# Four staging tiles and a later store for the last pair's differences in the down projections

## The chip, the cores and the metric

The kernel runs on one core of one Trainium2 chip. The metric is the device time of one execution in microseconds. Five engines work side by side, each through a queue of its own in order: TensorE (PE, with its weight loads PEld), VectorE (DVE), ScalarE (ACT), GpSimd (POOL) and SyncE (SP), which here only issues DMA transfers. An instruction whose semaphore isn't up yet holds back everything behind it on its engine's queue.

## The reference, cut to what matters

A decoder trunk with two layers over 1024 tokens of width 1024, each a mixer (retention and RWKV-7 in layer 0, windowed attention in layer 1) followed by a dense SwiGLU FFN with an inner width of 2816. The change touches only the end of the FFN:

```
def swiglu(h, w_gate, w_up, w_down):
    return (jax.nn.silu(h @ w_gate) * (h @ w_up)) @ w_down
...
    n = rms_norm(h, norm2_g[layer])
    h = h + swiglu(n, ffn_w_gate[layer], ffn_w_up[layer], ffn_w_down[layer])
```

Everything is float32.

## The kernel before, in words

**Arithmetic.** Each float32 operand is split into a rounded high half and a low half (an fp32r pair): ACT casts the high half, and DVE or POOL subtracts it from the source to get the low half. `prod` (lines 1297 to 1303) then issues three matmuls per 128x128 block, high by high (L1300), high by low (L1302) and low by high (L1303). The FFN's three products are taken over 2x2 blocks with seven block products in place of eight. For the down projection the blocks of the hidden values are: first or second inner tile of a pair, by first or second half of the tokens. There are 22 inner tiles of 128, so `NP` = 11 pairs. The sums and differences of blocks that the seven products need must be formed, split and kept: those of the hidden values are called the inner differences here.

**Inner differences.** `form_down(L, p, x, ts)` (line 1432) makes four of them for pair p. Its inner function `put(i, o, a, b)` subtracts on DVE (L1437), splits the result into a staging tile `t` (cast on ACT, L462; low half on POOL or, for the last pair, on DVE, L464), and has the tile stored to DRAM as `hc[L][p, i-1]` (512 KB, L1446 on SP's queue). The order of the puts is 1, 2, 4, 3. There are two staging tiles, `ts`: puts 1 and 4 use the first, puts 2 and 3 the second. So put 4's cast has to wait until put 1's store has read the tile, and put 3's cast until put 2's store has. `stage` (line 1412) makes the eight tiles of the late FFN: two staging tiles, two for each of the two sets `xs[0]` and `xs[1]` of hidden blocks (pairs take the sets in turn), and two for raw weights.

**When.** For pairs 0 to 9 `form_down` runs in the next pair's steps of the FFN (`ffn_late`, line 1854). For the last pair, 10, it runs as `rest` inside the down projection. `down` (line 1521) goes through three groups of pairs, (0 to 3), (4 to 7) and (8 to 10). In a group there are seven products, each over four output tiles `dp`:

| product | hidden operand | weights | PSUM tiles in group 0 (in group 1 the two sets are swapped) |
|---|---|---|---|
| 1 | first tile, first tokens, loaded plain from `hid` (L1502) and split | plain block | f, f, f, y |
| 2 | difference 2, loaded ready split from `hc` (L1497) | sums made by DVE (L1518) | m, m, r, c |
| 3 | second tile, first tokens, plain | plain block | f, f, f, y |
| 4 | difference 3 | sums | m, m, r, c |
| 5 | difference 4 | plain block | m, m, r, c |
| 6 | difference 1 | first sums, `s1` | f, f, f, y |
| 7 | second tile, second tokens, plain | second sums | f, f, f, y |

The weights come as raw halves into tiles `wd0` and `wd1` (L1510, five buffers each), are summed by DVE where needed, and are cast by ACT (L1491) and their low halves taken by POOL (L1492) into a ring of six tiles (`w`, and `wr`). The hidden operands take turns in twelve tiles (`n`, `ha`), four to a product, so an operand can be loaded when the product three before it is over.

**What sets the order.** A list scheduler orders each engine's queue by a timeline of its own, with the program's order as priority, save that the DMA issues marked with `keep` stay in program order among themselves. In program order a group's loads for products 1 to 7 come first to last; the transfers listed in `self.owed` are issued between the loads for product 5 and those for product 6 (line 1583, L1584), and `rest` stands after the loads for products 6 and 7 of group 0 (line 1592). The puts are held behind the last addition of product 5 by `self.rest`. Behind them on SP's queue stand the loads of group 1:

```
            X = [self.sums8(L, p, 4, place()) for p in ps]
            while self.owed:
                self.keep(self.nc.sync.dma_start(*self.owed.pop(0)))
...
            X = [self.sums8(L, p, 1, place()) for p in ps]
            X6 = [plain(1, 2 * p + 1) for p in ps]
            self.rest = self.last_vop
            for _ in rest:
                pass
```

Already before the change, `owed` carries three stores of the last pair's hidden values and two differences of pair 9. The first reader of `hc[L][10]` is product 2 of group 2.

## Time and profile before

| what | value |
|---|---|
| median of three runs | 2300.83 us (2300.7 to 2303.07) |
| profiled execution, its own time | 2298.91 us |
| profiled execution, span of the program in it | 2296.9 us |
| granted TensorE clock, mean | 0.998 |
| PE, DVE, ACT, POOL busy | 98%, 74%, 46%, 44% of the span |
| down projection of layer 0, products 2 of group 0 to 3 of group 2 | about 1119 to 1294 us |
| down projection of layer 1, the same | about 2080 to 2256 us |

The profile is one execution. The view of busy time by windows gives, for a stretch of the span, its length and then each engine's busy time with the number of instructions that touch the stretch. The view in order of time gives start, length, engine, line, operation, output and inputs; in square brackets stands how long the engine was idle before and what released it. Matmuls overlap in it: one is shown as 0.39 us long, while the next starts 0.22 to 0.23 us after it. For SP only the issue of a transfer is shown, and the landing is given apart. `SPq` is SP's queue.

### The profile page before, as it was taken

The page shows a single profiled execution, that of the slowest core. Times are in us where ns is not written, and L with a number is a line of the kernel's source. Part 1 is how long each engine was busy: PE and PEld are TensorE (multiplying, and loading weights), DVE is VectorE, ACT ScalarE, POOL GpSimd, SP SyncE. Part 2 cuts the span into 40 slices and gives each one's busy share as a digit, 9 for nine tenths or more (in the row PEclk, how much of TensorE's full clock was granted, in tenths as well). Part 3 has the DMA queues.
Part 4 walks back from the last instruction along what each step waited for, and adds up shares of the span by engine and source line. Part 5 has one row for each costly group of instructions (what it writes and reads, how often), then busy time and mean ns, then how long its engine had stood idle before and what let it go on. Part 6 is the DMA issues. An engine that isn't in the chain of part 4 may idle for free.

```text
span 2296.9 us, 35740 instructions
## 1 busy us (share of the span) xinstructions
PE 2261.4 (98%) x13056; PEld 1808.1 (79%) x13056; DVE 1694.1 (74%) x2635; ACT 1046.4 (46%) x1947; POOL 1007.3 (44%) x796
## 2 busy tenths in 40 slices
PE   8999999999999999999999999999999999999998
PEld 6777777778878888888878887787788888888786
DVE  7877965876567268887876958857657788888766
ACT  5454544424445333334333466657744333333335
POOL 3122221212340167777768501113203677777675
PEclk9999999999999999999999999999999999999999
DMA  8566554444356555565755332133246565556663
GB/s 279 190 211 207 195 160 132 141 117 132 134 183 224 170 175 202 207 216 210 284 234 202 114 119 74 44 106 110 92 147 225 178 215 208 205 193 252 259 218 115
DMA packets 170335, 406.42 MB, mean 177 GB/s; under 512 B 43184, under 2 KB 45872, under 8 KB 170160
## 3 DMA queue, kind: packets, MB, share of 16 engines
q1 hardware_dynamic: 166752, 397.59, 50.1%
q10 hardware_dynamic: 2832, 4.45, 0.5%
q8 instruction: 104, 1.70, 0.3%
q0 software_dynamic: 576, 2.10, 0.2%
q14 instruction: 71, 0.58, 0.1%
HBM read 275.48 MB, written 123.21 MB: 174 GB/s over the span
## 4 chain that ended last, share of the span: by engine, by line
PE 76%; DVE 11%; ACT 4%; DMA 4%; issue 3%; POOL 1%; SPq 1%; DVEq 0%; ACTq 0%; POOLq 0%
PE ps_f L293 11%; PE ps_m L1300 7%; PE ps_m L1302 7%; PE ps_m L1303 7%; PE ps_m L293 6%; PE ps_f L1300 4%; PE ps_f L1302 4%; PE ps_f L1303 4%; PE ps_f L450 2%; PE ps_f L447 2%; PE ps_f L449 2%; PE ps_r L1300 2%; PE ps_c L1303 2%; PE ps_r L1302 2%; PE ps_c L1302 2%
## 5 line engine op out<-in xcount | busy, mean ns | idle before, releaser
L293 PE MATMUL ps_f<-n,w 128*128 128x512 f32 x1440 | 358.5, 402 | 9.9 <-ACT w L432 5.8
L293 PEld LDWEIGHTS ps_f<-n,w 128*128 128x128 f32 x1440 | 267.1, 189 | 83.9 <-issue 12.6
L433 POOL TENSOR_TENSOR w<-wr,w 128x512 fp32r<-128x512 f32 x63 | 86.8, 1383 | 301.3 <-ACT w L432 299.8
L432 ACT CAST w<-wr 128x512 fp32r<-128x512 f32 x231 | 141.0, 617 | 162.0 <-PE ps_f L450 54.3
L433 DVE TENSOR_TENSOR w<-wr,w 128x512 fp32r<-128x512 f32 x168 | 118.3, 707 | 62.4 <-ACT w L432 61.8
L1300 PE MATMUL ps_f<-n,w 128*128 128x512 f32 x415 | 164.2, 396 | 0.0
L1302 PE MATMUL ps_f<-n,w 128*128 128x512 f32 x415 | 162.7, 392 | 0.0
L1303 PE MATMUL ps_f<-n,w 128*128 128x512 f32 x415 | 162.5, 392 | 0.0
L433 POOL TENSOR_TENSOR w<-wq,w 128x512 fp32r<-128x512 f32 x91 | 130.3, 1443 | 31.7 <-ACT w L432 31.7
L1300 PE MATMUL ps_m<-n,w 128*128 128x512 f32 x333 | 130.5, 392 | 1.3 <-DVE u L1310 1.3
L1302 PE MATMUL ps_m<-n,w 128*128 128x512 f32 x333 | 130.2, 391 | 0.5 <-POOL n L464 0.3
L1303 PE MATMUL ps_m<-n,w 128*128 128x512 f32 x333 | 129.6, 390 | 0.0
L1310 DVE TENSOR_TENSOR nq<-ps_m,u 128x512 f32<-128x512 f32 x88 | 58.8, 684 | 92.3 <-PE ps_m L1303 92.3
L1727 POOL TENSOR_SCALAR s<-s,st 128x256 f32<-128x256 f32 (+1 forms) x32 | 30.5, 952 | 191.8 <-ACT w L432 61.0
L1492 POOL TENSOR_TENSOR w<-wd,w 128x512 fp32r<-128x512 f32 (+1 forms) x62 | 87.0, 1415 | 45.6 <-ACT w L1491 32.6
L464 POOL TENSOR_TENSOR n<-nq,n 128x512 fp32r<-128x512 f32 x60 | 100.0, 1679 | 7.6 <-ACT n L462 7.6
L1300 PEld LDWEIGHTS ps_f<-n,w 128*128 128x128 f32 x415 | 77.9, 188 | 20.2 <-issue 3.8
L1300 PE MATMUL ps_m<-cb,w 128*128 128x512 f32 x236 | 91.9, 390 | 0.3 <-DVE nq L1310 0.3
L1303 PE MATMUL ps_m<-cb,w 128*128 128x512 f32 x236 | 91.8, 389 | 0.0
L1302 PEld LDWEIGHTS ps_f<-n,w 128*128 128x128 f32 x415 | 77.9, 188 | 17.6 <-issue 2.0
L1302 PE MATMUL ps_m<-cb,w 128*128 128x512 f32 x236 | 91.8, 389 | 0.0
L1303 PEld LDWEIGHTS ps_f<-n,w 128*128 128x128 f32 x415 | 77.9, 188 | 16.8 <-issue 0.7
(521 smaller groups left out, 6489.7 us busy)
## 6 DMA issues: line engine op xcount, KB each, us to landing
hc<-n SPq DMA_DIRECT2D x84, 512.0 KB, 3.0
wsp<-w SPq DMA_DIRECT2D x54, 512.0 KB, 3.2
w<-wsp SPq DMA_DIRECT2D x54, 512.0 KB, 3.4
n<-hc SPq DMA_DIRECT2D x54, 512.0 KB, 6.6
wq<-in_w_gate SPq DMA_DIRECT2D x44, 512.0 KB, 4.5
u<-u SPq DMA_DIRECT2D x88, 256.0 KB, 2.9
ha<-hc SPq DMA_DIRECT2D x34, 512.0 KB, 6.0
hid<-n SPq DMA_DIRECT2D x66, 256.0 KB, 2.0
```

The lines of the kernel that those rows point to most:

```text
L293: i = self.nc.tensor.matmul(out, lhsT, rhs, **kw)
L432: nc.scalar.copy(hi[:, :n], raw[:, c])
L433: self.lo.tensor_tensor(out=lo[:, :n], in0=raw[:, c], in1=hi.bitcast(F32)[:, :n], op=ALU.subtract)
L447: x = nc.tensor.matmul(ps, hi, rh, start=k == 0, stop=False)
L449: y = nc.tensor.matmul(ps, hi, rl, start=False, stop=False)
L450: z = nc.tensor.matmul(ps, lo, rh, start=False, stop=k == n - 1)
L464: e.tensor_tensor(out=lo, in0=src, in1=hi.bitcast(F32), op=ALU.subtract)
L1300: i = mm(ps, hi, xh, start=first and k == 0, stop=False, skip_group_check=True)
L1302: mm(ps, hi, xl, start=False, stop=False, skip_group_check=True)
L1303: mm(ps, lo, xh, start=False, stop=last and k == len(w) - 1, skip_group_check=True)
L1310: self.last_add = V.tensor_tensor(out=o, in0=x, in1=y, op=ALU.add)
L1492: nc.gpsimd.tensor_tensor(out=lo, in0=v, in1=hi.bitcast(F32), op=ALU.subtract)
```

## The change

`stage` gives each set of hidden blocks two more names, `11s` and `12s`, for its two whole tiles. `ffn_late` returns, beside the two staging tiles, the two tiles of the set that the last pair doesn't use (pair 9's, read for the last time by pair 9's own `form_down`). For the last pair each put takes a tile of its own, `ts[i - 1]`, and its store goes to the list `owed`, whichever put it is. At that time group 0 has emptied the list already, so the four stores are issued in group 1, between its loads for product 5 and for product 6. Pairs 0 to 9 are as they were. The number of matmuls, subtractions, casts, and bytes moved is the same.

```
-        return [{nm: t[4 - 2 * i + j // 2][:, j % 2, :] for j, nm in enumerate(names)} for i in range(2)], t[:2], [
+        xs = [{nm: t[4 - 2 * i + j // 2][:, j % 2, :] for j, nm in enumerate(names)} for i in range(2)]
+        for i, x in enumerate(xs):
+            x["11s"], x["12s"] = t[4 - 2 * i : 6 - 2 * i]
+        return xs, t[:2], [
...
-            t = ts[i in (2, 3)]
+            t = ts[i - 1] if p == NP - 1 else ts[i in (2, 3)]
             self.split(o, t[:, 0, :], t[:, 1, :], p < NP - 1)
             d = (self.hc[L][p, i - 1], t.bitcast(F32))
-            if p == NP - 2 and i > 2:
+            if p == NP - 1 or p == NP - 2 and i > 2:
                 self.owed.append(d)
...
-            return xs[(NP - 1) % 2], ts, X, W
+            old = [xs[NP % 2][nm + "s"].bitcast(F32R) for nm in ("11", "12")]
+            return xs[(NP - 1) % 2], ts + old, X, W
```

## The prediction

> **What bounds the kernel now.** I read the page first: the span, and how full TensorE is.

> ```profile
> span 2296.9 us, 35740 instructions
> ...
> PE 2261.4 (98%) x13056; PEld 1808.1 (79%) x13056; DVE 1694.1 (74%) x2635; ACT 1046.4 (46%) x1947; POOL 1007.3 (44%) x796
> ```

> PE is the bound, and no matmul goes away. So the change can only be worth the holes that it closes in PE's stream, and cost the holes that it opens. I looked for holes next, with the view of busy time by windows, cut at the borders of the products. In layer 0 the rows are products 5, 6 and 7 of group 0, then the first 108 matmuls of group 1 (products 1 and 2 and a quarter of 3), and last products 1 to 3 of group 2, which have 108 matmuls too. Below come the last two stretches for layer 1, with the 180 matmuls between them:

> ```profile
> 1152.40:1163.28 10.88, 10.88 (x49) 9.01 (x48) 10.57 (x10) 3.53 (x6) 9.40 (x7) 1.00 0.00 0
> 1163.28:1174.16 10.88, 10.88 (x49) 9.01 (x48) 10.69 (x13) 3.53 (x6) 5.32 (x3) 1.00 0.20 82
> 1174.16:1185.04 10.88, 10.88 (x49) 9.01 (x48) 3.67 (x7) 3.73 (x6) 2.77 (x2) 1.00 0.87 319
> 1185.04:1211.78 26.74, 25.72 (x110) 19.89 (x108) 23.25 (x25) 11.69 (x21) 19.92 (x14) 1.00 0.91 353
> ...
> 1263.46:1287.94 24.48, 24.48 (x110) 20.27 (x108) 21.49 (x26) 11.46 (x21) 14.21 (x14) 1.00 0.65 223
> ```

> ```profile
> 2146.61:2174.02 27.41, 25.74 (x110) 19.88 (x108) 22.86 (x25) 11.82 (x22) 20.06 (x14) 1.00 0.90 350
> 2174.02:2214.84 40.82, 40.82 (x181) 33.78 (x180) 25.14 (x31) 13.49 (x22) 34.54 (x23) 1.00 0.60 214
> ...
> 2225.72:2250.20 24.48, 24.48 (x109) 20.27 (x108) 19.85 (x24) 11.95 (x22) 14.13 (x14) 1.00 0.63 223
> ```

> The columns are length, then busy time and count of PE, PEld, DVE, ACT and POOL, then clock, DMA share and GB/s. Count by the weight loads: 108 matmuls take 24.48 us in group 2 of both layers, the pace of a full PE. The first 108 matmuls of group 1 take 26.74 and 27.41 us. So **the start of group 1 loses 2.26 us in layer 0 and 2.93 us in layer 1, together 5.19 us**. The start of group 2 loses nothing, and the clock is 1.00 throughout. The DMA columns give the hint: the DMA engines stand idle in product 5 (share 0.00), nearly so in product 6 (0.20), and then run full (0.87, 0.91) just when group 1 begins.

> Then I asked who fed PE late there (rows in order of time, PE of both layers, then what stands behind it):

> ```profile
> 1198.99 0.50 PE L1300 MATMUL ps_f<-ha,w 128*128 128x512 f32 x1 [0.93 <-ACT w L1491]
> ...
> 2147.33 0.50 PE L1302 MATMUL ps_m<-n,w 128*128 128x512 f32 x1 [0.33 <-POOL n L464]
> ...
> 2161.24 0.50 PE L1300 MATMUL ps_f<-ha,w 128*128 128x512 f32 x1 [1.25 <-ACT w L1491]
> ```

> ```profile
> 1189.19 0.92 DVE L1518 TENSOR_TENSOR ws<-wd 128x512 f32<-128x512 f32 x1 [2.10 <-DMA wd<-in_w_down]
> ...
> 1198.31 0.62 ACT L1491 CAST w<-ws 128x512 fp32r<-128x512 f32 x1 [2.40 <-DVE ws L1518]
> ```

> PE waited for a cast, the cast for a sum of weights on DVE, and the first such sum for its raw weights from DRAM. In layer 1 PE also waited for the low half of a plain operand. All of it is late loading. SP's queue says why:

> ```profile
> 1142.44 2.56 SPq L1502 DMA_DIRECT2D hr<-hid  x4
> 1168.54 8.40 SPq L1446 DMA_DIRECT2D hc<-n  x4
> 1177.00 0.42 SPq L1510 DMA_DIRECT2D wd<-in_w_down  x1
> 1177.52 2.16 SPq L1502 DMA_DIRECT2D hr<-hid  x4
> ```

> ```profile
> SPq L1446 <- DVE n L464: 30.0, 4, 23.1
> ```

> After the last loads of group 0, issued by 1145.00, SP stands for 23.1 us at the first of the last pair's four stores, and 30.0 us at all four, waiting for their low halves. Group 1's loads stand behind them and start at 1177.00, eight microseconds before group 1 does. Last, the casts of the last pair:

> ```profile
> 1171.21 0.62 ACT L462 CAST n<-nq 128x512 fp32r<-128x512 f32 x1 [1.61 <-DMA hc<-n]
> 1175.26 0.62 ACT L462 CAST n<-nq 128x512 fp32r<-128x512 f32 x1 [3.42 <-DMA hc<-n]
> ```

> These are puts 4 and 3, held by the stores of puts 1 and 2, whose tiles they overwrite.

> **The change part by part.**

> *Four tiles.* The two waits on ACT (1.61 and 3.42 us) go. PE ran full across them (10.88 us of 10.88 in products 6 and 7), so by themselves they are worth nothing to the end; they only let the last store, and SP, go some microseconds earlier. The tiles taken over belong to pair 9's set, which nothing reads after pair 9's differences; I count no new wait.

> *Stores leave SP's place before group 1.* This is the term that counts. SP then goes from 1145.00 straight to group 1's loads. What can hold them now? The first weight half has a free fifth buffer: at once. The four plain operands need the raw tiles of product 7's operands, the last of which DVE reads here:

> ```profile
> 1155.87 1.78 DVE L464 TENSOR_TENSOR n<-hr,n 128x512 fp32r<-128x512 f32 x1
> ```

> That is early in product 5. The other three first halves were last read in product 3. The second halves free up with product 5's casts. The differences for product 2 come free when product 6 ends, 1174.16. So the weights and plain operands land by about 1165 (my estimate from those borders), where now their issue begins at 1177.00: twenty microseconds ahead of use. DMA has room: shares of 0.00 and 0.20 there. The nearest case in the trace is group 2, whose loads weren't held by such stores: 0 us lost in 24.48 us, in both layers. Bounds for the gain are therefore 0 and 5.19 us; I take 5.19, the row of group 2 being the nearest, and keep both ends.

> *Stores reissued in group 1.* Rows of SP's queue around their new place in layer 0, and what such stores took elsewhere:

> ```profile
> 1206.79 2.36 SPq L1497 DMA_DIRECT2D ha<-hc  x4
> 1218.09 1.72 SPq L1497 DMA_DIRECT2D n<-hc  x3
> ```

> ```profile
> L1584 SPq DMA_DIRECT2D hc<-n x4: 490/557/640, 1132.6 to 2094.7; - x4
> ...
> DMA to landing us min/median/max: 7.5/8.0/9.1
> ```

> They go in after the four loads at 1206.79, which end at 1209.15. The queue then stands idle until 1218.09, that is 8.94 us. Four issues at up to 0.64 us take 2.56 us of it. Landing takes at most about 9.1 us, so by 1221. Their first reader is product 2 of group 2, after 1271 (products 1 to 3 start at 1263.46, and the first is a third of their 24.48 us). Cost 0. If that cover were gone, the four issues would put 2.56 us in front of product 6's loads, which have the rest of products 4 and 5 as slack. Nothing is queued behind a wait there: the halves have been ready since group 0.

> *Work that follows the loads.* Casts, splits and sums of group 1 come earlier: two low halves of product 1's operands on DVE and two on POOL move from the very start of group 1 into product 6 of group 0, where DVE is nearly full (10.69 of 10.88 us). Rows of DVE there, and PE's next use of the second bank:

> ```profile
> 1166.63 0.69 DVE L1437 TENSOR_TENSOR nq<-n,n 128x512 f32<-128x512 f32 x1
> ...
> 1168.44 1.78 DVE L1437 TENSOR_TENSOR nq<-n,nq 128x512 f32<-128x512 f32 x1
> ...
> 1172.44 0.68 DVE L1518 TENSOR_TENSOR h<-h,ps_f 128x512 f32<-128x512 f32 x1
> ```

> ```profile
> 1176.88 0.39 PE L1300 MATMUL ps_f<-n,w 128*128 128x512 f32 x1
> ```

> The same subtraction takes 0.69 us or 1.78 us. Product 7 may write its second bank (1176.88) only once DVE has read it (1173.12): a margin of 3.76 us. Two moved halves at up to 1.78 us use 3.56 us of it. I take 0 as the cost; the ends are 0 and the slower rival's price below.

> *Sum.* 0 − 5.19 + 0 + 0 = −5.19 us. The profiled execution took 2298.91 us, of which 2296.9 us are the span; that would be 2293.7 us. The median of the runs lies 1.92 us above that execution, so the forecast for it is 2300.83 − 5.19 = **2295.6 us**, −0.23%. What PE gains in layer 0 is passed on, since all later work depends on it and PE is 98% busy.

> [...]

> **The rivals.**

> *Only part of the stall goes.* DVE may not sum group 1's weights before product 7's additions (the code holds them behind these), so the two waits for a cast could stay even with early loads. They are 0.93 and 1.25 us in the rows above, 2.18 us. For it: that order is in the code. Against it: group 2 has it too and lost nothing, though its operands are three pairs wide, not four. Time: −(5.19 − 2.18) = −3.0, so 2297.8 us.

> *The loads stay late, or the gain comes out elsewhere.* The change moves the stores but the loads wait for something that now hides behind them, such as the raw tiles or the ring of twelve; then the start of group 1 is as before. For it: DMA's idle stretch in product 5 proves only the stores' wait, not what comes next. Against: the borders worked out above. Time: 0, so 2300.8 us.

> *Slower: DVE's queue in product 6.* The queues are ordered anew. If the moved halves and the two puts that no longer wait stand ahead of DVE's read of the second bank, PE waits at product 7. Price: DVE has 10.69 us of work in product 6; with two halves more at 1.78 us and its nine short instructions stretched by 1.09 us each (1.78 − 0.69) it has 24.1 us, against 10.88 + 3.76 = 14.6 us of room: 9.4 us per layer. At the other end, the two halves alone, 3.56 us, it still fits. The point that decides is 3.76 us of added delay before that read; a net loss starts where both layers wait over 5.19 us together, so at about 6.4 us of added delay. Between that break-even, 2.6 us per layer, and the upper end, 9.4 us, the middle is 6.0 us: 12.0 − 5.19 = +6.8, so 2307.6 us. Upper end: 18.8 − 5.19 = +13.6, so 2314.4 us. For it: DVE is full there, and the order is the scheduler's. Against it: in group 1, the same splits before group 2 cost nothing (40.82 us for 180 matmuls is the full pace), though there are no puts among them.

> **How the numbers follow.** A measurement of this kernel tells about 0.2% from no change, 4.6 us, that is under 2296.2 or over 2305.4 us. Chances: forecast 0.42, part 0.24, none 0.16, slower 0.18. The forecast lies just beyond the bound, so 0.02 of it falls short. Faster 0.40, same 0.02 + 0.24 + 0.16 = 0.42, slower 0.18. The range reaches from 2293.0 (the forecast with 2.6 us of spread, about the 2.4 us that the three runs differ by) to 2303.0 (no gain, with 2.2 us), and leaves out the slower rival. Since cases of both signs are in, the forecast's own range is 2293.0 to 2297.0 us.

> **What would show it.** Right: SP's first load of group 1 right after 1145 in layer 0 and before product 5 ends in layer 1; DMA share well above 0.00 in product 5; no ACT wait for a store of `hc`; 108 matmuls in about 24.5 us at the start of group 1; four stores of `hc` issued by L1584 in group 1. Wrong: the same 26.7 and 27.4 us there (loads still late); waits for ACT casts but none for POOL's halves (the part); a new wait of PE on DVE in product 7 (the slower rival); or a difference outside the down projections, which would mean that the reordering of queues outweighs all of this.

## The result and the profile after

| | before | changed |
|---|---|---|
| median, first measurement, 5 runs each | 2300.83 us | 2292.58 us (2290.52 to 2295.7) |
| ratio to before, 95% interval | | 0.9961 [0.9949, 0.9972] |
| median, second measurement, 35 and 11 runs | 2299.89 us | 2293.56 us |
| ratio to before, 95% interval | | 0.9974 [0.9963, 0.9984] |
| profiled execution, its own time and its span | 2298.91, 2296.9 us | 2295.7, 2293.9 us |

The kernel became faster, by 8.25 us in the first measurement and about 6 us in the second. The forecast was 2295.6 us and the range ended at 2293.0, so the first measurement lies 0.42 us below it. Single runs of the kernel before scatter over 10 us (2296.01 to 2306.28 in 35 runs), so I rest what follows on stretches of the profile, which repeat much better, and use the medians to check their sum.

First the page of the changed kernel: the same matmuls, a little more of the span filled by PE.

```profile
span 2293.9 us, 35742 instructions
...
PE 2261.0 (99%) x13056; PEld 1810.2 (79%) x13056; DVE 1698.6 (74%) x2635; ACT 1047.1 (46%) x1947; POOL 1006.5 (44%) x796
```

Next the view of busy time by windows of the changed kernel. Layer 0's products 5, 6 and 7 of group 0, the first 108 matmuls of group 1 and of group 2; in the last row the first 108 matmuls of layer 1's group 1. Columns as in the prediction.

```profile
1156.03:1166.91 10.88, 10.88 (x50) 9.01 (x48) 10.58 (x10) 5.26 (x9) 9.87 (x8) 1.00 0.55 166
1166.91:1177.79 10.88, 10.88 (x50) 9.01 (x48) 10.85 (x14) 5.01 (x10) 6.68 (x5) 1.00 0.76 290
1177.79:1188.67 10.88, 10.88 (x50) 9.01 (x48) 10.69 (x11) 4.44 (x8) 8.33 (x7) 1.00 0.77 270
1188.67:1213.15 24.48, 24.48 (x110) 20.27 (x108) 23.46 (x24) 8.11 (x15) 17.37 (x11) 1.00 0.41 130
1264.83:1289.31 24.48, 24.48 (x110) 20.27 (x108) 22.03 (x27) 11.35 (x22) 14.25 (x14) 1.00 0.65 224
2146.59:2171.07 24.48, 24.48 (x109) 20.27 (x108) 23.05 (x25) 7.91 (x15) 17.55 (x11) 1.00 0.44 132
```

The start of group 1 now takes 24.48 us in both layers, the pace of group 2, to the hundredth. It took 26.74 and 27.41. The DMA share (last column but one) shows why: 0.55 in product 5, where it was 0.00, and 0.41 at the start of group 1, where it was 0.91. The transfers moved ahead of their use.

SP's queue in the changed kernel, around the end of group 0 in layer 0, and the place where the stores went:

```profile
1145.95 2.51 SPq L1505 DMA_DIRECT2D hr<-hid  x4
1148.50 0.47 SPq L1513 DMA_DIRECT2D wd<-in_w_down  x1
1157.36 4.74 SPq L1505 DMA_DIRECT2D hr<-hid  x4
1162.14 4.38 SPq L1513 DMA_DIRECT2D wd<-in_w_down  x7
1175.94 2.36 SPq L1500 DMA_DIRECT2D ha<-hc  x4
```

```profile
1208.58 2.36 SPq L1500 DMA_DIRECT2D ha<-hc  x4
1211.03 2.89 SPq L1587 DMA_DIRECT2D hc<-n  x4
1219.46 2.36 SPq L1500 DMA_DIRECT2D n<-hc  x4
```

All of this execution runs some 3.6 us later than that of before (product 5 begins at 1156.03, not 1152.40; the last section says why). The first weight half goes out right behind the last loads of group 0, at 1148.50. The other loads of product 1 wait for free tiles, no longer for stores, and are all issued by 1166.52, which is 22 us before group 1 begins; in before they began 8 us before it. Product 2's differences follow at 1175.94, when tiles of the ring come free. In layer 1 it is the same. The four stores take 2.89 us of SP's idle time at 1211. SP's waits at this line (the second row, 0.4 us in each layer, belongs to the last pair's stores, the first to a store of group 0 in layer 1), and how long all stores by this line took to land:

```profile
SPq L1587 <- DVE h L1521: 0.9, 1, 0.9
SPq L1587 <- DVE y L1521: 0.8, 2, 0.4
```

```profile
DMA to landing us min/median/max: 7.7/8.2/9.9
```

So SP loses 0.4 us at them, in time in which it is idle anyway. The last one is issued at 1213.49 and in DRAM by 1223. The loads that bring the differences back for product 2 of group 2, one for each of its three pairs, go out 20 us later at the earliest:

```profile
1243.26 0.33 SPq L1500 DMA_DIRECT2D ha<-hc  x1
1252.10 1.00 SPq L1500 DMA_DIRECT2D n<-hc  x2
```

Last, the last two casts of the four puts on ACT, and DVE's reads of product 6's second and third bank, then the read of the third bank in before:

```profile
1175.83 0.62 ACT L462 CAST n<-nq 128x512 fp32r<-128x512 f32 x1 [1.87 <-DVE nq L1440]
1176.88 0.61 ACT L462 CAST n<-nq 128x512 fp32r<-128x512 f32 x1
```

```profile
1176.92 0.68 DVE L1521 TENSOR_TENSOR h<-h,ps_f 128x512 f32<-128x512 f32 x1
...
1180.53 0.68 DVE L1521 TENSOR_TENSOR h<-h,ps_f 128x512 f32<-128x512 f32 x1
```

```profile
1173.64 0.68 DVE L1518 TENSOR_TENSOR h<-h,ps_f 128x512 f32<-128x512 f32 x1
```

No cast of the last pair waits for a store any more; one waits for its own subtraction. DVE's read of the second bank ends at 1177.60, that is 10.69 us after product 6 began (1166.91). In before it ended 9.84 us after (1173.12 and 1163.28). The work that moved used up 0.85 of the 3.76 us of margin there. At the third bank it used up more: its read ends at 1181.21, and product 7 writes this bank from 1183.23 on, a margin of 2.02 us, where before had 5.28 (1174.32 and 1179.60). Layer 1 has 2.02 us there too.

The full sum of what differs: 2.26 us in layer 0 and 2.93 in layer 1, which I had, and **1.38 us at a place that I did not have**, in layer 1's late FFN, long before its down projection. Here is that stretch in before, then in the changed kernel:

```profile
1950.06:2000.08 50.02, 48.75 (x214) 39.82 (x213) 43.33 (x46) 18.04 (x31) 36.09 (x25) 1.00 0.55 198
```

```profile
1951.49:2000.13 48.64, 48.64 (x215) 39.82 (x213) 41.98 (x46) 18.21 (x31) 36.46 (x25) 1.00 0.58 202
```

The same 213 matmuls, in the same order on every engine, and PE lost 1.27 us in before and nothing after. DVE's busy time fell from 43.33 to 41.98 us for the same 46 instructions. The puts that run there are those of earlier pairs, which the change leaves as they were.

### The profile page after: what moved, and what is told of

It reads as the page before. It is cut to its first block, busy times and chain, and to the rows that moved or that the text cites. A ratio compares the mean times of both kernels' runs of the same rounds, so it can differ in the third digit from the quotient of the medians.

```text
span 2293.9 us, 35742 instructions
## 1 busy us (share of the span) xinstructions
PE 2261.0 (99%) x13056; PEld 1810.2 (79%) x13056; DVE 1698.6 (74%) x2635; ACT 1047.1 (46%) x1947; POOL 1006.5 (44%) x796
## 4 chain that ended last, share of the span: by engine, by line
PE 77%; DVE 10%; ACT 5%; DMA 3%; issue 3%; SPq 1%; POOL 1%; DVEq 0%; ACTq 0%; POOLq 0%
PE ps_f L293 9%; PE ps_m L1300 7%; PE ps_m L1303 7%; PE ps_m L1302 7%; PE ps_m L293 6%; PE ps_f L1300 5%; PE ps_f L1302 5%; PE ps_f L1303 5%; PE ps_f L450 2%; PE ps_f L447 2%; PE ps_f L449 2%; PE ps_r L1300 2%; PE ps_c L1303 2%; PE ps_r L1303 2%; PE ps_r L1302 2%
## 5 line engine op out<-in xcount | busy, mean ns | idle before, releaser
L1300 PE MATMUL ps_f<-n,w 128*128 128x512 f32 x415 | 164.2, 396 | 0.0
L1302 PE MATMUL ps_f<-n,w 128*128 128x512 f32 x415 | 162.7, 392 | 0.0
L1300 PE MATMUL ps_m<-n,w 128*128 128x512 f32 x333 | 130.4, 392 | 0.0
L1302 PE MATMUL ps_m<-n,w 128*128 128x512 f32 x333 | 129.6, 389 | 0.0
L464 POOL TENSOR_TENSOR n<-nq,n 128x512 fp32r<-128x512 f32 x60 | 100.1, 1681 | 7.6 <-ACT n L462 7.6
L1300 PEld LDWEIGHTS ps_f<-n,w 128*128 128x128 f32 x415 | 77.9, 188 | 20.2 <-issue 3.8
L1300 PE MATMUL ps_m<-cb,w 128*128 128x512 f32 x236 | 91.9, 389 | 0.4 <-DVE nq L1310 0.4
L1302 PEld LDWEIGHTS ps_f<-n,w 128*128 128x128 f32 x415 | 77.9, 188 | 17.7 <-issue 2.0
L1302 PE MATMUL ps_m<-cb,w 128*128 128x512 f32 x236 | 91.8, 389 | 0.0
```

What stands on the lines that cost most here:

```text
L464: e.tensor_tensor(out=lo, in0=src, in1=hi.bitcast(F32), op=ALU.subtract)
L1300: i = mm(ps, hi, xh, start=first and k == 0, stop=False, skip_group_check=True)
L1302: mm(ps, hi, xl, start=False, stop=False, skip_group_check=True)
```

## The experiments

Theory A is the prediction's: SP's queue is what matters, the four tiles are worth nothing by themselves. Rival B: the tiles matter too, because the waits that they remove stand in the chain that leads to the stores. For the 1.38 us the theories were formed on the way. The table gives medians, ratios with their intervals, and three stretches of each kernel's profile: the first 108 matmuls of group 1 in both layers, and layer 1's late FFN.

| kernel | median us (runs) | ratio to before, 95% | layer 0 | layer 1 | late FFN |
|---|---|---|---|---|---|
| before, again | 2299.99 (11) | 1.0004 [0.9995, 1.0014] | 27.04 | 27.72 | 50.01 |
| changed, again | 2293.56 (11) | 0.9974 [0.9963, 0.9984] | 24.48 | 24.48 | 48.65 |
| four tiles only | 2296.48 (11) | 0.9983 [0.9973, 0.9992] | 24.83 | 25.48 | 50.00 |
| stores on POOL's queue only | 2296.32 (12) | 0.999 [0.9981, 0.9998] | 25.46 | 26.38 | 48.67 |
| change in layer 0 only | 2296.71 (11) | 0.9988 [0.9979, 0.9997] | 24.48 | 27.48 | 48.63 |
| change in layer 1 only | 2298.72 (11) | 0.9994 [0.9985, 1.0003] | 27.19 | 24.48 | 50.04 |
| late stores only | 2293.42 (6) | 0.9971 [0.996, 0.9982] | 24.48 | 24.48 | 48.66 |
| four tiles, stores on POOL's queue | 2292.55 (6) | 0.9969 [0.9958, 0.998] | 24.48 | 24.48 | 48.66 |

**The kernel before and the changed one, again.** No edit. They show how far the stretches and the medians repeat.

> The kernel before, unchanged, timed against itself. Scatter theory (the 3 us by which the change gained more than the 5.19 us of its two stretches are chance events of single executions outside the down projections): single runs spread over 4 us or more, the median stands within 2 us of the other copy, and the profile shows such events at other places than the first profile did. Elsewhere theory (the 3 us are a standing effect of the newly ordered queues behind group 0): the first 108 matmuls of group 1 again take 26.7 and 27.4 us, and PE again waits 1.27 us for DVE in the late FFN of layer 1 at about 1962 us.

> The changed kernel a second time, on another chip run. Scatter theory: again 5 to 8 us faster, the amount not the same as the 8.25 us of the first time; 24.48 us for the first 108 matmuls of group 1 in both layers. Elsewhere theory: again 8 us faster, with the stretch between the two down projections again 1.4 us shorter than in the kernel before.

The stalls of before vary by 0.3 us between its two profiles (in the kernels with copies below, which leave them alone, they take up to 27.42 us in layer 0 and once 28.69 in layer 1), the late FFN by 0.01 us. The change repeats its stretches to 0.01 us, and its gain is smaller by the medians, 6.3 us, than in the first measurement. The stretches sum up to 6.57 us, which lies in both intervals. So each of the two theories holds in part: the 1.4 us of the late FFN are a standing effect, and what the first measurement gained beyond 6.57 us didn't come again.

**Four tiles only.** The tiles of the change, with the stores at once on SP's queue (edit against the changed kernel).

```
             t = ts[i - 1] if p == NP - 1 else ts[i in (2, 3)]
...
-            if p == NP - 1 or p == NP - 2 and i > 2:
+            if p == NP - 2 and i > 2:
```

> Four tiles, but the last pair's stores issued at once on SP's queue, ahead of group 1's loads, as before. Queue theory (the gain comes from group 1's loads no longer standing behind the stores): no ACT wait for a store any more, the four stores issued by about 3 us earlier, group 1's loads still not before 1172, so most of the loss stays: 25.3 to 26.5 us for the first 108 matmuls in layer 0, 26 to 27 us in layer 1, and 1 to 2.5 us faster in all. Tiles theory (the gain comes from the two waits of ACT): 24.5 us in both layers and 5 us or more faster.

SP's queue of this kernel in layer 0, and the two starts of group 1:

```profile
1142.38 2.51 SPq L1505 DMA_DIRECT2D hr<-hid  x4
1168.38 5.72 SPq L1449 DMA_DIRECT2D hc<-n  x4
1174.15 0.59 SPq L1513 DMA_DIRECT2D wd<-in_w_down  x1
```

```profile
1184.88:1209.71 24.83, 24.81 (x110) 20.19 (x109) 21.82 (x23) 10.81 (x20) 18.25 (x13) 1.00 0.88 345
2144.36:2169.84 25.48, 25.14 (x110) 20.04 (x108) 21.91 (x25) 11.28 (x21) 17.73 (x12) 1.00 0.90 348
```

SP still stands at the first store until 1168.38, but the four stores take 5.72 us, not 8.40, and group 1's first load goes out at 1174.15, which is 10.73 us before group 1 begins, not 8.04. These 2.69 us were enough for 1.91 and 1.93 us of the stalls. **Theory A falls in this point**: the casts' waits for stores were no loss to PE where they stood, but the longer one was a link of a chain (store of put 2, cast of put 3, its low half, its store, SP, group 1's loads) that ended in PE's stall.

**Stores on POOL's queue only.** Two tiles as in before; the last pair's stores leave SP's queue (edit against before).

```
-                (nc.gpsimd if p == NP - 2 else nc.sync).dma_start(*d)
+                (nc.gpsimd if p >= NP - 2 else nc.sync).dma_start(*d)
```

> Two tiles as before, the last pair's four stores issued at once but on POOL's queue instead of SP's. Queue theory: group 1's loads start right after 1145 in layer 0, the two ACT waits for stores stay (1.6 and 3.4 us or a little longer), and the first 108 matmuls of group 1 still take 24.5 us in both layers: 5 us faster, less what POOL loses by four issues of 0.6 us and by waiting for the last pair's low halves. Tiles theory: 26.7 and 27.4 us stay, no gain.

The first weight load on SP, the last two puts' casts on ACT, and the landing of layer 0's four stores in this kernel, then the same in before:

```profile
1143.32 0.33 SPq L1510 DMA_DIRECT2D wd<-in_w_down  x1
```

```profile
1174.06 0.62 ACT L462 CAST n<-nq 128x512 fp32r<-128x512 f32 x1 [3.67 <-DMA hc<-n]
1181.06 0.62 ACT L462 CAST n<-nq 128x512 fp32r<-128x512 f32 x1 [6.38 <-DMA hc<-n]
```

```profile
DMA to landing us min/median/max: 2.9/5.4/7.7
```

```profile
DMA to landing us min/median/max: 2.6/2.6/3.0
```

The loads are as early as in the changed kernel, and yet 0.98 us of layer 0's stall and 1.90 of layer 1's stay (25.46 and 26.38, less 24.48). Now the stores, issued from 1169.96 to 1183.55, stand among loads that went out early (SP issues eight more from 1170.40 to 1174.76), and take up to 7.7 us to land where they took 3.0 at most. That the loads slow them is my reading of these times; POOL's queue by itself isn't the reason, since before's four stores on it, for pair 9, landed in 2.9 to 3.1 us. The casts that must wait for them stand 3.67 and 6.38 us (1.61 and 3.42 in before), with group 1's casts of weights behind them on ACT's queue. So with SP's queue free the two waits still cost PE time, now through ACT's queue. The two parts alone recover 3.84 and 2.31 us, 6.15 in all, more than the 5.19 that there were: they overlap, and neither is a term that can be added.

**Both, in two other ways.** Four tiles with the stores at once on POOL's queue (edit against the changed kernel):

```
-            if p == NP - 1 or p == NP - 2 and i > 2:
+            if p == NP - 2 and i > 2:
...
-                (nc.gpsimd if p == NP - 2 else nc.sync).dma_start(*d)
+                (nc.gpsimd if p >= NP - 2 else nc.sync).dma_start(*d)
```

> Four tiles, and the four stores issued at once on POOL's queue: both parts without the later place. Both-parts theory: 24.5 us for the first 108 matmuls of group 1 in both layers, as with the change, and 5 us or more faster; no ACT wait for a store. If the later place in SP's queue matters by itself (the stores taking DMA time from group 1's loads), some of the loss stays, 25 us or more.

and two tiles with the stores in group 1 (edit against before). In this kernel two of the four stored differences are others than the reference's (puts 4 and 3 have overwritten the tiles by then), so it has no wait of a cast for a store, and its time is that of the late place alone:

```
-            if p == NP - 2 and i > 2:
+            if p == NP - 1 or p == NP - 2 and i > 2:
```

> Two tiles as before, but all four stores issued a group later on SP's queue. Queue theory alone: group 1's loads start right after 1145 and 24.5 us for its first 108 matmuls. Both-parts theory (early loads need the four tiles, since otherwise the casts of the third and fourth difference wait for the stores, and ACT's later casts behind them): these two casts wait until the stores are issued in product 2 or 3 of group 1, PE waits for casts or sums there, and the stretch takes more than 26.7 us or its loss moves into products 3 to 5; no gain or slower.

Both have 24.48 us in both layers, and their ratios, 0.9969 and 0.9971, can't be told from the changed kernel's. So the later place as such is worth nothing, nor do the four issues on POOL cost anything. What counts is that **no load of group 1 stands behind a last pair's store, and no cast waits for one**.

**One layer at a time.** The change where `L == 0` (edit against the changed kernel); the other kernel has `L == 1` in the same places:

```
-            t = ts[i - 1] if p == NP - 1 else ts[i in (2, 3)]
+            t = ts[i - 1] if p == NP - 1 and L == 0 else ts[i in (2, 3)]
...
-            if p == NP - 1 or p == NP - 2 and i > 2:
+            if p == NP - 1 and L == 0 or p == NP - 2 and i > 2:
```

> The whole change, in layer 0 alone. Queue and tiles together: 24.48 us for the first 108 matmuls of group 1 in layer 0, 27.4 us in layer 1. Standing theory (the shorter stretch in layer 1's late FFN, 48.65 for 50.0 us, is carried there from the new order in layer 0): it is 48.65 us here too, and the kernel is 2.3 + 1.4 = 3.7 us faster. Chance theory: that stretch may be 50.0 or 48.65 us, and the kernel is 2.3 us faster.

> The whole change, in layer 1 alone. 26.7 us for the first 108 matmuls of group 1 in layer 0, 24.48 us in layer 1. Standing theory: the stretch of layer 1's late FFN stays at 50.0 us, as its instructions stand before the change, and the kernel is 2.9 us faster. Chance theory: the stretch may come out at 48.65 us.

Each closes its own layer's stall and leaves the other's as it was. The late FFN of layer 1 is short with layer 0's part and long with layer 1's. So the 1.38 us come from what the change does in layer 0, some 760 us earlier.

**What in layer 0 does it?** In all long kernels ACT's cast `w<-ws` near 1950 us starts about 0.36 us after the matmul that releases it; in the short ones some 0.08 us after. Counted from ACT's first instruction (number 0, waiting instructions included), that cast is number 2367 in before and 2369 in the changed kernel, which has two waiting instructions more ahead of it. The other kernels of the table fit: 2367 in before again, with four tiles only and with layer 1 only, all long; 2369 to 2373 in the rest, all short. Late starts of 0.36 us were at the numbers 1215, 1343, 1599, 2239, 2367 and 2495 of ACT in one kernel or another, whatever instruction had the number: in before at 1215 and 2367, in the changed kernel at 2367, there the cast `w<-n` at 1949.29 (0.35 us). Theory P (position): the instruction at such a number starts late, and the change moved the number off the cast. Rival T (timing): earlier transfers of layer 0 shift what follows. To tell them apart, N copies of 128x16 into an unused tile stand on ACT at the start of layer 1's mixer, in before or in the changed kernel; up to 65 of them leave the order of everything else as it was (with 127 and more, a few neighbouring instructions of the mixer change places).

```
+        z = self.t(ap, [P, 16], "z")
+        for _ in range(N):
+            nc.scalar.copy(z, self.pv[:, :16])
         self.pk = self.pvt = None
```

> Before, with two copies of 128x16 on ACT at the start of layer 1's mixer, into a tile that nothing reads. The order of all engines is otherwise that of before. Theory (position): on ACT, an instruction whose number in the queue ends a block of 64 starts some 0.28 us late; the two copies move that from the cast of the weight sum at about 1950 us to an instruction two places earlier, as the change's additional waits do. Then layer 1's stretch from about 1950 to 2000 us takes 48.65 us, not 50.0, the stalls at the start of group 1 stay at 26.7 to 27.0 and 27.4 to 27.7 us, and the whole is about 1.4 us faster (0.9994). Rival (timing): the stretch gets shorter because the earlier loads of layer 0 shift all that follows; then two copies do nothing and it stays at 50.0 us.

> Before, with 64 such copies in the same place. Position: 64 is a whole block, so the same cast is hit again and the stretch takes 50.0 us, as in before. If merely having more ACT work in the mixer, or another phase, made the stretch shorter, it would take 48.65 us here too. The stalls at the start of group 1 stay as before.

> The changed kernel with 62 such copies in the same place: with the two additional instructions that stand ahead of the cast in the changed kernel they make a whole block of 64. Position: the stretch takes 50.0 us again, though the start of group 1 is at the full 24.48 us in both layers. Timing: the loads of layer 0 are as early as in the changed kernel, so it stays at 48.65 us.

> Before, with 65 copies on ACT at the start of layer 1's mixer. In the trace of the kernel with 64 copies one waiting instruction of ACT is gone, so the cast near 1950 us came 63 places later, not 64, and had number 2430 (62 beyond a multiple of 64); the stretch took 48.64 us. With 65 copies it comes 64 places later, number 2431 (63 beyond). Position: the cast starts late again and the stretch takes 50.0 us. Timing, or any effect of the amount of ACT work: as with 64 copies, 48.65 us.

> The changed kernel with 63 copies there. With 62 copies the cast had number 2430 and the stretch took 48.63 us; one copy more makes it 2431, again 63 beyond a multiple of 64. Position: the stretch takes 50.0 us, with the start of group 1 at 24.48 us in both layers. Timing: 48.65 us, as in the changed kernel and with 62 copies.

> Before, with 129 copies on ACT at the start of layer 1's mixer. In all traces so far ACT's late starts of about 0.36 us lie on numbers that leave 63 when divided by 128 (1215, 1343, 1599, 2239, 2367, 2495), so a block is 128 instructions, not 64; 65 copies put the cast on 2431, which leaves 127, and it wasn't late. With 129 copies the cast comes 128 places later, number 2495. Position with blocks of 128: the cast starts about 0.36 us after its release and the stretch takes 50.0 us. Timing, or the amount of ACT work: 48.65 us, as with 2, 64 and 65 copies.

> The changed kernel with 127 copies there: its cast near 1950 us has number 2369 without them, and with 126 places more 2495. Position with blocks of 128: the stretch takes 50.0 us although the start of group 1 stays at 24.48 us in both layers. Timing: 48.65 us, as in the changed kernel without copies.

> Before, with 130 copies on ACT at the start of layer 1's mixer. With 129 copies two waiting instructions went, so the cast had number 2494 and the waiting instruction behind it 2495; that one came 0.30 us after the cast's start, where with 65 copies it came 0.02 us after. With one copy more the cast itself has number 2495. Position with blocks of 128: the cast starts about 0.36 us after its release and the stretch takes 50.0 us. Timing, or the amount of ACT work: 48.6 us, as with 129 copies.

> The changed kernel with 128 copies there: with 127 the cast had number 2494 and the stretch took 48.63 us. Position with blocks of 128: the cast has number 2495 and the stretch takes 50.0 us, although the start of group 1 stays at 24.48 us in both layers. Timing: 48.63 us, as with 127 copies.

| kernel, N | number of the cast | late FFN us | group 1, layers 0 and 1 |
|---|---|---|---|
| before, 0 | 2367 = 18 x 128 + 63 | 50.02 | 26.74, 27.41 |
| before, 2 | 2369 | 48.65 | 26.84, 27.28 |
| before, 64 | 2430 | 48.64 | 27.42, 27.41 |
| before, 65 | 2431 = 18 x 128 + 127 | 48.67 | 26.83, 27.24 |
| before, 129 | 2494 | 48.61 | 27.08, 28.69 |
| before, 130 | 2495 = 19 x 128 + 63 | 50.03 | 27.08, 27.64 |
| changed, 0 | 2369 | 48.64 | 24.48, 24.48 |
| changed, 62 | 2430 | 48.63 | 24.48, 24.48 |
| changed, 63 | 2431 = 18 x 128 + 127 | 48.66 | 24.48, 24.48 |
| changed, 127 | 2494 | 48.63 | 24.48, 24.48 |
| changed, 128 | 2495 = 19 x 128 + 63 | 50.01 | 24.48, 24.48 |

Two copies bring the gain without the change (their median of 10 runs, 0.9994 [0.9985, 1.0004], is too coarse to tell 1.4 us). Then I missed twice. I had taken the step for 64; with 65 and 63 copies the cast stood exactly 64 places behind 2367, on 2431, and started on time, so steps of 64 fell. The numbers above fit 128 as well. And the copies took one or two waiting instructions with them, which I counted only after the runs with 64, 62, 129 and 127. With 130 and 128 copies the cast has number 2495, and the long stretch is back in both kernels, though in the changed one the start of group 1 stays at 24.48 us. One copy less, and it is short. T says nothing of this. **P holds, with steps of 128.**

How 0.28 us become 1.38: the late FFN by windows in the changed kernel with 127 copies and with 128, then rows of the first (second fence) and of the second (third fence), by engine.

```profile
1950.64:1999.27 48.63, 48.63 (x215) 39.82 (x213) 41.98 (x46) 18.16 (x31) 36.46 (x25) 1.00 0.57 203
...
1950.72:2000.73 50.01, 48.74 (x215) 39.82 (x213) 43.33 (x46) 18.03 (x31) 36.09 (x25) 1.00 0.54 197
```

```profile
1950.90 0.63 ACT L432 CAST w<-ws 128x512 fp32r<-128x512 f32 x1 [2.11 <-PE ps_m L1303]
...
1951.95 1.50 DVE L1440 TENSOR_TENSOR nq<-n,nq 128x512 f32<-128x512 f32 x1
...
1956.78 0.68 DVE L1440 TENSOR_TENSOR nq<-n 128x512 f32<-128x512 f32 x1
...
1956.81 1.80 POOL L433 TENSOR_TENSOR w<-ws,w 128x512 fp32r<-128x512 f32 x1 [0.50 <-ACT w L432]
```

```profile
1951.26 0.62 ACT L432 CAST w<-ws 128x512 fp32r<-128x512 f32 x1 [2.39 <-PE ps_m L1303]
...
1952.03 1.77 DVE L1440 TENSOR_TENSOR nq<-n,nq 128x512 f32<-128x512 f32 x1
...
1957.12 1.77 DVE L1440 TENSOR_TENSOR nq<-n 128x512 f32<-128x512 f32 x1
...
1956.89 1.45 POOL L433 TENSOR_TENSOR w<-ws,w 128x512 fp32r<-128x512 f32 x1 [0.24 <-ACT w L432]
...
1963.04 0.47 PE L1300 MATMUL ps_m<-n,w 128*128 128x512 f32 x1 [1.27 <-DVE u L1310]
```

The cast waits 2.39 us, not 2.11. POOL, which follows it, is late, and the first subtraction beside it takes 1.77 us, not 1.50. So DVE reaches the next one 0.27 us later in relation to POOL. With 127 copies DVE starts it 0.03 us ahead of POOL and takes 0.68 us, while POOL's instruction is drawn out to 1.80. With 128 POOL is 0.23 us ahead, takes 1.45, and DVE's subtraction 1.77. DVE loses 0.27 + 1.09 = 1.36 us, and PE waits 1.27 us for DVE. The same rows stand in before (1.77 and 1.77). In each of these two races the instruction that started first took the shorter of its two times, and the other the longer: 0.68 against 1.77 us on DVE, 1.45 against 1.80 on POOL, for a difference of 0.26 us in arrival.

## Why the prediction was wrong, and where it was right

The step that failed is the *Sum*, together with the range around it: it put nothing outside the two starts of group 1, and the runs show 1.38 us in layer 1's late FFN. The first measurement lies 3.06 us below the forecast. Those 1.38 us are one part of it; the other 1.68 us are in no stretch that I found and didn't come again in the second measurement. Either part alone would have stayed inside the range.

- **What bounds the kernel: right.** The stalls were 5.19 us, they stood where the prediction put them, and SP's queue was the cause.
- ***Stores leave SP's place before group 1*: right in its size** for the change as a whole: all 5.19 us came, by the full pace of group 1. The loads went out 22 us ahead of use, where I had put them landed 20 us ahead; with the 6 to 10 us that loads of weights take there, the last landed at 1175.59, 13 us ahead of use. My borders were too early, without effect.
- ***Four tiles*: this is the step that failed in its reasoning.** "By themselves they are worth nothing to the end" came from PE's being full across the two waits. Measured, they recover 3.84 of 5.19 us by themselves, and without them the freed queue recovers only 2.31. I had written down the path ("they only let the last store, and SP, go some microseconds earlier") and not priced it: the 3.42 us that put 3's cast waited stood in the chain that ended in stalls of 2.26 and 2.93 us. The forecast didn't suffer, but by luck: I gave all 5.19 us to the stores' new place, and they needed the tiles, which were in the change for no gain of their own that I had counted.
- ***Stores reissued in group 1*: right**, 2.89 us of SP's idle time, and no reader waits. Their first readers in DRAM are the loads from 1243.26 to 1253.10, though, not product 2 after 1271.
- ***Work that follows the loads*: right in its cost of 0,** not in the place to watch. PE is full through products 5 to 7, so the slower rival fell. No run shows its upper end's nine short instructions of DVE stretched by 1.09 us each: in product 6 of the changed kernel eight still take 0.67 or 0.68 us. I had looked at the second bank, where 0.85 us of 3.76 went; the third lost 3.26 of 5.28 us and became the closest, with 2.02 us left. DVE's busy time in product 6 can't show this, since it filled the 10.88 us in both kernels (10.69, then 10.85); the rest of the work stands in product 7 (3.67, then 10.69).
- **The rival "only part of the stall goes" fell, and so did "the loads stay late".** DVE did sum the weights in time, as in group 2.
- ***Sum*: this is where the number failed first.** It had no term for 1.38 us of the late FFN. The step "Wrong: ... or a difference outside the down projections" named that case without giving it a price or a place in the range. With the term the forecast would be 2300.83 − 6.57 = 2294.3 us. I couldn't have worked it out from the change, but the profile of before did show the late cast, the two subtractions at 1.77 us and PE's wait of 1.27 us, so a loss that any shift of ACT's queue might remove was there to be found.
- **The range** gave the lower end 2.6 us for the spread of the runs. A median of five runs of a kernel that scatters over 10 us needed more: the first measurement is 1.7 us beyond what the stretches hold, the second 0.2 us short of it. I take this rest for scatter in code that is the same in both (the last section has its largest known place); no run pins it down.

## What to carry to other kernels

A wait that doesn't stop the bounding engine where it stands can still be a link in the chain that does so later: follow it to the next transfer or queue before writing 0. When two parts of a change loosen the same chain, try each alone; their gains overlap, and one may need the other (here free tiles are needed once the queue is free, because stores among the early loads took up to 7.7 us to land, not 3.0). And look for near-ties between DVE and POOL in the profile of before: here 0.26 us in arrival decided 1.09 us of DVE's time, and an edit of two copies on ACT flipped it (48.65 us for the late FFN, not 50.02).

## What the runs showed of the hardware

**The clock after a hole.** The scatter has one large known place, in layer 0's mixer, before anything that the change touches. PE's rows there in before, then in the changed kernel:

```profile
283.36 3.24 PE L293 MATMUL ps_f<-n,w 128*128 128x512 f32 x13 [2.58 <-DVE n L579]
```

```profile
284.58 5.91 PE L293 MATMUL ps_f<-n,w 128*128 128x512 f32 x13 [3.25 <-DVE n L579]
```

And the window of these 13 matmuls in the changed kernel:

```profile
284.58:290.49 5.91, 5.91 (x15) 4.19 (x17) 5.77 (x15) 0.00 (x0) 0.06 (x1) 0.50 0.52 154
```

After a hole of 3.25 us the same 13 matmuls take 5.91 us at a granted clock of 0.50; in before, after 2.58 us, they take 3.24 at 1.00. Together with the longer hole this cost the profiled execution of the changed kernel about 3 us (the matmuls that take 99.99 us from 200 us on in before took 103.05), and is most of why its timeline runs late by 3.6 us. In other runs they took 3.23 to 5.92 us: 3.26 after a hole of 2.12 us in before again, but 4.84 at a clock of 0.65 after 2.14 us with late stores only, and 4.85 at 0.65 after 2.12 us with 129 copies. So the lower clock came after holes of 2.12 to 3.25 us, and not after every such hole: behind 2.58 us they took 3.24 us in before and 4.84 in the kernel with two copies. What decides between the two, no run here shows.
